# The last plain block of the down product: its loads tied to a place in the queue, its splits spaced otherwise, and the last scaling read from PSUM

## The chip, the cores and the metric

The kernel runs on 1 core of a Trainium2 chip. The metric is device time in microseconds (us), the median of 3 runs. TensorE (PE) multiplies, VectorE (DVE), ScalarE (ACT) and GpSimd (POOL) do everything elementwise, and every transfer is issued by SyncE (SP), in one queue and in order.

## The reference, cut to what matters

One step of a two-layer decoder. The first layer is a Mamba-2 mixer, the second is sliding-window attention, and each is followed by a squared-ReLU MLP. All is float32. The change touches the down product of the MLPs, the output product of the mixer (they share code) and the final norm.

```python
def rmsnorm(x, w):
    xf = x.astype(jnp.float32)
    xf = xf * lax.rsqrt(jnp.mean(xf * xf, axis=-1, keepdims=True) + EPS)
    return (xf * w.astype(jnp.float32)).astype(x.dtype)

def sq_relu_mlp(h, norm_w, w_up, w_down):
    return h + jnp.square(jax.nn.relu(rmsnorm(h, norm_w) @ w_up)) @ w_down
...
    y_prompt = rmsnorm(hp, final_norm_w)
    y_sample = rmsnorm(hs, final_norm_w)
```

## The kernel before, in words

The stream is kept transposed, features on the 128 partitions and tokens in columns (1104 columns in the first layer, 1088 in the second). A float32 operand is multiplied as two fp32r parts, hi and lo, with three matmuls per product (`mm3`, lines 204 to 206). To make the parts ("a split") ACT copies the tile to fp32r (hi) and DVE subtracts that from the tile (lo).

The down product sums over 4096 hidden features in blocks. The first and the last block of 512 features are plain products (`down_block`, tile `R0`, called R in the trace). The six tiles of features between them go as 4 blocks through `block_products`: seven products in place of eight for each 2x2 cut. A place in it is written (b, p, i): block b of 4 (of 2 in the mixer), weight group p of 4, product i of 7. Each (b, p) takes two loads of weights (`down_weights`, line 1160), which are added, subtracted and split (lines 1166 to 1172, 1047, 1048), and each product is added to the stream or to a sum by DVE (line 1264), which frees its PSUM bank. Each block needs seven split operands. They are loaded by `load` (line 1224) and split by `parts` (lines 1229, 1230) around the border of two blocks: a slot can be loaded again only when the block before has made its last product with it. Seven operands and the spare memory of R0 turn in a ring: the third block keeps two operands in R0, at its products i = 2 and i = 3 of p = 3.

The last block's `step` also fetches the data of the last plain block into R0: `last[0]` is `block_load`, four loads (line 1140) of a quarter each, numbered j = 0 to 3 here, and `last[1](j)` is `block_parts(j)`, the split of one quarter (ACT line 1145, DVE line 1146). The lo parts of quarters 0 and 1 lie where the second of the two operands in R0 was, those of 2 and 3 lie in memory that nothing uses during `block_products`; the hi parts of all four lie over the two operands.

The order on an engine is not the order of the text. The program is built with `schedule_with_timeline_sim=True`: a scheduler places each instruction, earlier in the text first, as soon as a model of the time says that its inputs and its memory are ready. `tc.issue_after(ins)` adds an edge of order alone: what the block issues on the engine of `ins` comes behind `ins` in its queue. It is used with `self.last_raw` in two places: the loads of the stream (line 1133) and one copy from memory to memory, `out_dram<-in_cache_v_dram` (line 1425). In the kernel before, `last_raw` is set by the up product's weight loads alone (line 1041).

At the very end the last plain block goes through `down(tail=2)`: the last four of eight feature tiles u are made chunk by chunk (three chunks c of 384, 384 and 320 columns), and `final` follows each tile: squares summed on ACT and DVE; `final_rs` sums over partitions with one-column matmuls (line 1726), takes root (1728) and reciprocal (1729) and makes diagonal matrices `dg` (1732); `final_bc` spreads the factor over the partitions with matmuls (1743) into PSUM and copies it to SBUF (`rs`, 1745); `final_scale` multiplies (1755 with the norm's weight as well, 1758 without) and stores (1759). For chunks 0 and 1 the eight multiplications go to POOL and DVE, four each; for chunk 2 to DVE six, to POOL two. POOL reads `rs` in SBUF. DVE reads `rs` too for chunks 0 and 1, and PSUM for chunk 2.

Of the kernel before, what the change touches and what calls it, by code (L numbers as in the profile page):

```python
# [93 lines left out]
class Stream:  # L94
# [29 lines left out]
    def load(self, X):  # L124

        self.X = X
        for c in self.rs:
            self.k.nc.sync.dma_start(out=X[:, :, self.cols(c)], in_=self.h_d[:, :, self.cols(c)])
        for c in list(self.rs):
            self.norm(c)  # L130
# [11 lines left out]
class Kernel:  # L142
# [1010 lines left out]
    def down_weights(self, view, p):  # L1153

        nc = self.nc
        sh = [KB, P]
        raws = []
        for j in range(2):
            t = self.np.tile([P, 2, KB, P], F32, tag="n3", bufs=2, name="raw") if p % 2 else self.raw([P, 2, KB, P])
            nc.sync.dma_start(out=t, in_=view[p, :, j])  # L1160
            raws.append(t)
        (a11, a12), (a21, a22) = ((t[:, 0], t[:, 1]) for t in raws)

        def add(a, b, op):
            t = self.np.tile([P] + sh, F32, tag="n1", bufs=5, name="s")
            nc.vector.tensor_tensor(out=t, in0=a, in1=b, op=op)
            return t
        yield self.wparts(a11, sh)
        s1 = add(a21, a22, ALU.add)
        yield self.wparts(s1, sh)  # L1170
        d = add(a11, a21, ALU.subtract)
        nc.vector.tensor_tensor(out=s1, in0=s1, in1=a11, op=ALU.subtract)  # L1172
        yield self.wparts(d, sh)
        yield self.wparts(s1, sh)
        yield self.wparts(a12, sh)
        yield self.wparts(a22, sh)
        yield self.wparts(add(a12, s1, ALU.subtract), sh)
# [55 lines left out]
    def block_products(self, w, big, us, slots, load, parts, free, make, last, more, early=(0, 0)):  # L1233


        nc = self.nc
        nn = us.shape[2]
        qw = nn // 2
        nb = len(slots)
        h = [[big[:, 4 * j:4 * j + 4, i * nn:i * nn + nn] for i in range(2)] for j in range(2)]  # L1240

        def step(b, p, i):

            if b == nb - 1:
                if (p, i) == (0, 0):
                    last[0]()
                if p > 0 and i == 2:
                    last[1](p - 1)
                if p == 3 and i == 5:
                    last[1](3)  # L1250
            else:
                for k in range(2):
                    if i == 0 and p == early[k]:
                        load(b + 1, k)
                if p in (1, 2) and i == 2:
                    parts(b + 1, p - 1)
                if p == 3 and i in free[b]:
                    load(b + 1, free[b].index(i) + 2)
                if p == 3 and i in make[b]:
                    parts(b + 1, make[b].index(i) + 2)  # L1260
            if p == 0 and b and i + 7 in make[b - 1]:
                parts(b, make[b - 1].index(i + 7) + 2)

        tt = lambda out, x, y: nc.vector.tensor_tensor(out=out, in0=x, in1=y, op=ALU.add)  # L1264
        for b in range(nb):
            for p in range(4):
                banks = {}
                hv = [[h[j][i][:, p] for i in range(2)] for j in range(2)]
                uv = us[:, p]
                for i, (wh, wl) in enumerate(self.down_weights(w[b], p)):  # L1270
                    e = self.CHAIN[p % 2][i]
                    new = e not in banks
                    if new:
                        banks[e] = self.pq.tile([P, 1024], F32, tag=e, bufs=1, name="m" + e)
                    x = [(hi[:, q], lo[:, q]) for hi, lo in slots[b][i] for q in range(lo.shape[1])]
                    for k in range(2):
                        cs = slice(k * qw, k * qw + qw)
                        self.mm3(banks[e][:, 512 + (k - 1) * qw:512 + k * qw], [(wh[:, q], wl[:, q]) for q in range(KB)],
                                 [(hi[:, cs], lo[:, cs]) for hi, lo in x], new)
                    pv = banks[e][:, 512 - qw:512 + qw]  # L1280
                    to = (uv, hv[1][1], hv[1][1], uv, hv[0][0], hv[1][0], hv[0][1])[i]
                    if i == 0 and b == 0:
                        nc.scalar.copy(out=uv, in_=pv)
                    else:
                        tt(to, pv, to)
                    if b == nb - 1 and i in (3, 4, 5):
                        e, to = ((nc.gpsimd, hv[1][1]), (nc.gpsimd, hv[0][1]), (nc.vector, hv[1][0]))[i - 3]
                        e.tensor_tensor(out=to, in0=to, in1=uv, op=ALU.add)
                    step(b, p, i)
                    more(b, p, i)  # L1290
# [445 lines left out]
    def final_bc(self, c, chs):  # L1736

        nc = self.nc
        n = chs[c][1]
        ps = self.gps()[:, :n]  # L1740
        for b in range(3):
            o = min(b * P, n - P)
            nc.tensor.matmul(out=ps[:, o:o + P], lhsT=self.ones_d, rhs=self.acc[c][:, b], start=True, stop=True)
        rs = self.fin("rs", 2, n)
        nc.scalar.copy(out=rs, in_=ps)
        self.acc[c] = {nc.gpsimd: rs, nc.vector: ps if c == 2 else rs}

    def final_scale(self, c, k, e, hts, chs):
        nc = self.nc
# [277 lines left out]
```

## Time and profile before

| | us |
|---|---|
| median of 3 runs | 2924.53 |
| lowest, highest | 2918.5, 2924.64 |
| profiled execution | 2923.57 |
| its span, first to last instruction | 2921.9 |
| PE busy in it | 2816.2 (96%) |
| DVE busy | 1895.0 (65%) |

Times in the trace count from the first instruction of the span. A row of a wait says who waited, for whom, how long in total, how often and how long at most. `x` is a count. Where PE has no row of a wait, it ran.

### The profile page before, as it was taken

To read this page: it belongs to the slowest core of one execution; us is meant where nothing else is said; L and a number is where in the kernel's file an instruction comes from. 1 tells how busy PE (TensorE), PEld (TensorE's weight loads), DVE (VectorE), ACT (ScalarE), POOL (GpSimd) and SP (SyncE) were. 2 spreads that over 40 slices of the span, in tenths; PEclk is the share of its full clock that TensorE was granted. 3 is DMA by queue.
4 is the path that set the end of the run, shared out by engine and by line. 5 is a ranking of instruction groups with operands and counts; after the bars stand their busy time and mean duration, and the time that the engine had idled before them with its cause. 6 is when DMAs were issued, how large, how long until landed. Compare 5 with 4: busy or idle time off the path is not lost.

```text
span 2921.9 us, 51729 instructions
## 1 busy us (share of the span) xinstructions
PE 2816.2 (96%) x19895; PEld 2711.0 (93%) x19895; DVE 1895.0 (65%) x2995; ACT 1413.9 (48%) x2742; POOL 1386.1 (47%) x1279
## 2 busy tenths in 40 slices
PE   8999999988989999999999999999999999999998
PEld 6999999978889999999999999988889999999998
DVE  6788777765657675455466765666678454356675
ACT  6555555544555264444343325655555444433333
POOL 5566666665546615444266573312112444345562
PEclk9999999999999999999999999999999999999998
DMA  3344544447655224444554422447453444533422
GB/s 137 91 128 124 125 128 123 123 123 258 218 206 171 80 85 149 136 156 139 224 212 171 161 89 94 160 153 261 164 187 133 150 140 150 206 138 124 151 96 73
DMA packets 219470, 433.43 MB, mean 148 GB/s; under 512 B 30728, under 2 KB 128392, under 8 KB 216648
## 3 DMA queue, kind: packets, MB, share of 16 engines
q1 hardware_dynamic: 219224, 430.14, 44.3%
q8 instruction: 156, 2.56, 0.4%
q14 instruction: 90, 0.74, 0.1%
HBM read 302.71 MB, written 128.32 MB: 148 GB/s over the span
## 4 chain that ended last, share of the span: by engine, by line
PE 77%; DVE 10%; ACT 4%; issue 3%; DMA 3%; POOL 3%; SPq 0%; DVEq 0%; ACTq 0%; POOLq 0%
PE g L204 10%; PE g L206 10%; PE g L205 10%; PE mc L204 4%; PE mc L206 3%; PE mc L205 3%; PE ma L204 3%; PE ma L205 3%; PE ma L206 3%; PE md L206 3%; PE md L205 3%; PE md L204 3%; PE mb L206 3%; PE mb L204 3%; PE mb L205 3%
## 5 line engine op out<-in xcount | busy, mean ns | idle before, releaser
L1048 POOL TENSOR_TENSOR w<-s,w 128x384 fp32r<-128x384 f32 (+1 forms) x272 | 370.4, 1368 | 386.9 <-ACT w L1047 354.4
L206 PE MATMUL g<-S,w 128*128 128x384 f32 (+2 forms) x1584 | 531.1, 336 | 3.9 <-POOL w L171 3.3
L204 PE MATMUL g<-S,w 128*128 128x384 f32 (+2 forms) x1584 | 533.4, 337 | 1.3 <-DVE qp L1462 0.6
L205 PE MATMUL g<-S,w 128*128 128x384 f32 (+2 forms) x1584 | 533.6, 337 | 0.0
L1048 POOL TENSOR_TENSOR w<-raw,w 128x384 fp32r<-128x384 f32 (+1 forms) x204 | 264.3, 1301 | 286.2 <-ACT w L1047 255.2
L171 POOL TENSOR_TENSOR w<-raw,w 128x1024 fp32r<-128x1024 f32 x96 | 247.1, 2574 | 253.3 <-ACT w L170 189.3
L206 PEld LDWEIGHTS g<-S,w 128*128 128x128 f32 x1584 | 301.9, 191 | 5.8 <-POOL w L171 3.6
L204 PEld LDWEIGHTS g<-S,w 128*128 128x128 f32 x1584 | 301.3, 190 | 4.7 <-issue 1.5
L205 PEld LDWEIGHTS g<-S,w 128*128 128x128 f32 x1584 | 301.7, 190 | 0.9 <-issue 0.3
L1047 ACT CAST w<-s 128x384 fp32r<-128x384 f32 (+1 forms) x272 | 149.8, 557 | 313.0 <-DVE s L1172 84.7
L204 PE MATMUL ma<-S,w 128*128 128x276 f32 (+1 forms) x808 | 235.2, 291 | 8.0 <-DVE us L1264 6.7
L206 PE MATMUL ma<-S,w 128*128 128x276 f32 (+1 forms) x808 | 234.7, 290 | 0.0
L205 PE MATMUL ma<-S,w 128*128 128x276 f32 (+1 forms) x808 | 234.3, 290 | 0.0
L1047 ACT CAST w<-raw 128x384 fp32r<-128x384 f32 (+1 forms) x204 | 111.8, 555 | 154.6 <-PE mc L206 45.2
L602 DVE SCALAR_TENSOR_TENSOR fm<-xp,cv,fm 128x1024 f32<-128x1024 f32 x96 | 162.8, 1698 | 33.1 <-ACT fm L583 32.5
L204 PEld LDWEIGHTS ma<-S,w 128*128 128x128 f32 x808 | 153.3, 190 | 9.3 <-ACT S L1229 2.7
L205 PE MATMUL g<-R,w 128*128 128x384 f32 (+2 forms) x480 | 158.6, 330 | 0.0
L204 PE MATMUL g<-R,w 128*128 128x384 f32 (+2 forms) x480 | 158.1, 329 | 0.0
L206 PE MATMUL g<-R,w 128*128 128x384 f32 (+2 forms) x480 | 158.1, 329 | 0.0
L205 PEld LDWEIGHTS ma<-S,w 128*128 128x128 f32 x808 | 153.5, 190 | 0.0
L206 PEld LDWEIGHTS ma<-S,w 128*128 128x128 f32 x808 | 153.2, 190 | 0.0
L170 ACT CAST w<-raw 128x1024 fp32r<-128x1024 f32 x96 | 100.5, 1047 | 105.8 <-DMA raw<-in_w_o_dram 19.9
(492 smaller groups left out, 8696.0 us busy)
## 6 DMA issues: line engine op xcount, KB each, us to landing
raw<-in_w_up_dram SPq DMA_DIRECT2D x64, 512.0 KB
raw<-in_w_in_dram SPq DMA_DIRECT2D x48, 512.0 KB
raw<-in_w_downs_dram SPq DMA_DIRECT2D x64, 384.0 KB
w<-ws_o SPq DMA_DIRECT2D x48, 512.0 KB
w<-ws_q SPq DMA_DIRECT2D x40, 512.0 KB
ab<-acs_d SPq DMA_DIRECT2D x64, 256.0 KB
S<-t_d SPq DMA_DIRECT2D x18, 828.0 KB
S<-t_e SPq DMA_DIRECT2D x18, 816.0 KB
```

Of the source, the lines that this page charges most:

```text
L170: nc.scalar.copy(out=wh, in_=raw)
L171: nc.gpsimd.tensor_tensor(out=wl, in0=raw, in1=wh.bitcast(F32), op=ALU.subtract)
L204: mm(out=out, lhsT=wh, rhs=xh, start=(first and k == 0), stop=False)
L205: mm(out=out, lhsT=wh, rhs=xl, start=False, stop=False)
L206: mm(out=out, lhsT=wl, rhs=xh, start=False, stop=(k == n - 1))
L602: nc.vector.scalar_tensor_tensor(out=acc[:, :SEQ], in0=xp[:, k:k + SEQ], scalar=cv[:, j, k:k + 1], in1=acc[:, :SEQ], op0=ALU.mult, op1=ALU ...
L1047: nc.scalar.copy(out=t[:, 0], in_=src)
L1048: nc.gpsimd.tensor_tensor(out=t[:, 1], in0=src, in1=t[:, 0].bitcast(F32), op=ALU.subtract)
```

## The change

The four loads of the last plain block move from (last b, 0, 0) to (last b, 1, 0), and get an edge of order behind `last_raw`, which is now also set by `down_weights`: there it is the second weight load of p = 1 of the last block. The four splits move from (1, 2), (2, 2), (3, 2), (3, 5) to (1, 3), (2, 2), (2, 5), (3, 2), in the form (p, i). The three callers of `block_products` (mixer, first and second layer) share this. In `final_bc`, DVE's factor is the tile in PSUM for every chunk.

```diff
             t = self.np.tile([P, 2, KB, P], F32, tag="n3", bufs=2, name="raw") if p % 2 else self.raw([P, 2, KB, P])
-            nc.sync.dma_start(out=t, in_=view[p, :, j])
+            self.last_raw = nc.sync.dma_start(out=t, in_=view[p, :, j]).ins
...
             if b == nb - 1:
-                if (p, i) == (0, 0):
-                    last[0]()
-                if p > 0 and i == 2:
-                    last[1](p - 1)
-                if p == 3 and i == 5:
-                    last[1](3)
+                if (p, i) == (1, 0):
+
+                    with self.tc.issue_after(self.last_raw):
+                        last[0]()
+                if p > 0 and i in ((3,), (2, 5), (2,))[p - 1]:
+                    last[1](p - 1 if i < 4 and p < 3 else p)
...
         nc.scalar.copy(out=rs, in_=ps)
-        self.acc[c] = {nc.gpsimd: rs, nc.vector: ps if c == 2 else rs}
+        self.acc[c] = {nc.gpsimd: rs, nc.vector: ps}
```

## Rows read from the trace of the kernel before

**Rows 1.** The page, busy time of each engine, share of span, instructions

```profile
PE 2816.2 (96%) x19895; PEld 2711.0 (93%) x19895; DVE 1895.0 (65%) x2995; ACT 1413.9 (48%) x2742; POOL 1386.1 (47%) x1279
```

**Rows 2.** Waits of PE in 860:1000, 1400:1760, 2560:2922: total us, times, longest

```profile
PE mc L204 <- DVE hh L1264: 1.8, 2, 1.0
...
PE ma L204 <- DVE us L1264: 4.9, 2, 2.5
PE mb L204 <- DVE hh L1264: 4.8, 1, 4.8
PE ma L204 <- DVE hh L1264: 3.4, 3, 1.2
...
PE g L1743 <- DVE dg L1732: 4.4, 2, 3.5
PE mb L204 <- DVE hh L1264: 2.6, 1, 2.6
...
PE ma L204 <- DVE us L1264: 1.8, 2, 0.9
...
PE md L205 <- DVE S L1230: 1.1, 1, 1.1
```

**Rows 3.** Timeline of SP's queue, 2586:2592 and 2766:2812: start us, us, line, transfer

```profile
2588.95 0.36 SPq L1140 DMA_DIRECT2D R<-r_e  x1
...
2768.25 2.58 SPq L1160 DMA_DIRECT2D raw<-in_w_downs_dram  x2
2771.18 2.35 SPq L1224 DMA_DIRECT2D A<-t_e  x2
2777.72 0.93 SPq L1140 DMA_DIRECT2D R<-r_e  x2
```

**Rows 4.** Timeline of ACT around the last block's start, layer 2 (2775:2784), layer 1 (1650:1664)

```profile
2775.46 1.11 ACT L1145 CAST R<-R 128x1088 fp32r<-128x1088 f32 x1 [1.56 <-PE mc L205]
...
2781.57 1.11 ACT L1145 CAST R<-R 128x1088 fp32r<-128x1088 f32 x1 [0.26 <-DMA R<-r_e]
2782.89 1.11 ACT L1145 CAST R<-R 128x1088 fp32r<-128x1088 f32 x1 [0.21 <-DMA R<-r_e]
...
1656.83 1.58 ACT L1229 CAST A<-A 128x1656 fp32r<-128x1656 f32 x1 [4.87 <-DMA A<-t_d]
```

**Rows 5.** Groups of DVE by form, 2775:2811: count, busy us, mean ns, idle before

```profile
L1146 DVE TENSOR_TENSOR R<-R 128x1088 fp32r<-128x1088 f32 x4 | 6.7, 1695 | 0.3 <-ACT R L1145 0.3
```

**Rows 6.** Groups of DVE by form in the final norm, 2890:2922

```profile
L1755 DVE SCALAR_TENSOR_TENSOR hh<-hh,nv,rs 128x384 f32<-128x384 f32 x4 | 5.5, 1407 | 0.8 <-ACT rs L1745 0.8
L1758 DVE TENSOR_TENSOR hh<-hh,rs 128x384 f32<-128x384 f32 x4 | 5.3, 1355 | 0.0
...
L918 DVE TENSOR_TENSOR hh<-hh,g 128x384 f32<-128x384 f32 x3 | 1.7, 553 | 1.7 <-PE g L206 1.5
...
...
L1755 DVE SCALAR_TENSOR_TENSOR hh<-hh,nv,g 128x320 f32<-128x320 f32 x2 | 1.0, 546 | 1.9 <-ACT rs L1745 1.9
```

**Rows 7.** Timelines of DVE and ACT at the end (2896:2918, 2899:2916)

```profile
2911.94 0.16 DVE L1729 RECIPROCAL rt<-rt 128x3 f32<-128x3 f32 x1
...
2909.03 0.26 ACT L1728 ACTIVATE rt<-g,eps 128x3 f32<-128x3 f32 x1 [2.30 <-PE g L1726]
```

**Rows 8.** Timeline of PE at the end (2902.8:2915)

```profile
2902.57 0.31 PE L206 MATMUL g<-R,w 128*128 128x320 f32 x1
2903.83 0.94 PE L1743 MATMUL g<-dg,ones_r 128*128 128x128 f32 x6 [0.94 <-DVE dg L1732]
2906.31 0.54 PE L1726 MATMUL g<-ones_r,acc 128*128 128x1 f32 x2 [1.55 <-DVE acc L1705]
...
2912.48 1.65 PE L1743 MATMUL g<-dg,ones_r 128*128 128x128 f32 x6 [3.49 <-DVE dg L1732]
```

**Rows 9.** Stretch 2906.5:2912: busy us of PE, PEld, DVE, ACT, POOL, granted clock, DMA

```profile
2906.50:2912.00 5.50, 2.49 (x12) 2.40 (x12) 5.24 (x5) 0.49 (x2) 4.80 (x4) 0.50 0.29 105
```

**Rows 10.** Timeline of SP's queue, 1366:1373

```profile
1368.28 0.86 SPq L1425 DMA_DIRECT2D out_dram<-in_cache_v_dram  x1
```

## The prediction

> **What bounds the kernel now.** I read the page first, then PE's waits stage by stage, then the queues around the longest waits. PE is busy 96% of the span [rows 1], so time is won only where PE stands still, or after its last product. The waits in the three stages that the change touches are few [rows 2]. Ahead of the last block of `block_products` PE waits 1.8 us in the mixer, 4.8 + 1.2 = 6.0 in the first layer (1.2 is the longest of three in its row) and 2.6 + 1.1 = 3.7 in the second, together 11.5 us. All end with DVE: it adds a product to the stream too late to free a bank, or splits an operand too late. The borders between earlier blocks, which have seven splits but none of R, cost 2.5 + 1.1 = 3.6 us each in the first layer and at least 0.9 each in the second. So DVE is short of time at every border, and the four splits of R, 6.7 us of DVE at the last one in the second layer [rows 5], come on top there. The second place is the end: PE waits twice for `dg`, 4.4 us [rows 2], and the reciprocal ahead of it starts at 2911.94, although the root that it takes ended at 2909.29 [rows 7]. In between DVE multiplied chunk 1.
>
> **The factor from PSUM.** Four multiplications of 384 columns by DVE per chunk stay, for chunks 0 and 1; their second operand moves from SBUF to PSUM. They take 1.407 and 1.355 us now, beside POOL, which multiplies from SBUF in the same time (4.80 us for its four). An addition of the same 384 columns with one operand in PSUM takes 0.553, and a multiplication with the weight, 320 columns, 0.546, also beside POOL [rows 6, 9]. I take 0.553 for two and 0.546 x 384/320 = 0.655 for the other two: 2.4 us a chunk in place of 2 x 1.407 + 2 x 1.355 = 5.5. The start does not move: chunk 2, which reads PSUM already, waits 1.9 us for ACT's copy all the same [rows 6]. The PSUM bank is held 2.4 us instead of one copy, and comes round again only seven tiles later, after the products in between: no cost while those last longer.
>
> On the path it counts in two steps. Chunk 0: its multiplications end 3.1 us sooner, and the additions of chunk 2's tiles behind them on DVE move up with them, until they meet the products themselves. PE's last product ends at 2902.88; one addition of at most 0.55, one square on ACT of about as much, and the last sums can start at some 2904.0 in place of 2906.31 [rows 6, 8]: 2.3 us. Chunk 1: its four then end before the root of chunk 2 does, so the reciprocal follows the root at once: 2911.94 - 2909.29 = 2.65 us [rows 7]. Behind them all is as before: diagonals, matmuls, copy, DVE's six, stores. Sum: 4.95 us. POOL does not come late: its 4.80 us [rows 9] start 2.3 us sooner too and end near 2909.4, ahead of chunk 2's copy. The lower bound is 2.65, if chunk 0 gains nothing. Upwards: in the last stretch the granted clock is 0.50 of full speed, that is 1.2 GHz, after PE had idled 0.94 and 1.55 us, and six matmuls that took 0.94 us at 2903.83 take 1.65 at 2912.48 [rows 8, 9]. With shorter idling it may stay at 2.4 GHz longer; 0.7 for these six and about 1.2 for the twelve ahead of them give an upper bound of 6.9.
>
> The Trainium skill speaks against this edit: "VectorE: DVE Perf Modes", section "Rules for kernel authors", says to accept the plain rate from PSUM, or to copy to SBUF first if many operations read it. By that rule the copy that the kernel makes anyway should be read, and the edit would gain nothing. The row of 0.553 against 1.355 says otherwise, and "SBUF — State Buffer", section "SBUF: two separate sides", has a reason: a DVE instruction with two SBUF inputs and GpSimd share a port that one holds for a whole instruction.
>
> **The loads and splits.** What decides is whether the splits leave the border. The order is not the text's. Quarters 2 and 3, written into the last block, are loaded at 2588.95, about 190 us ahead, as soon as their memory is free (the other one follows); and the first split runs at 2775.46, at the very moment PE finishes with the operand under its hi part, though the text has all four in the second to fourth group of the last block, which has not begun then [rows 3, 4]. So the place in the text is only a rank among what is ready, and I expect nothing of the new places by themselves. What binds is the edge. But the load it points to is early: weights are fetched almost two groups ahead, and the second weight load of (last, p = 1) is the second of the pair at 2768.25 to 2770.83. Quarters 0 and 1 are at 2777.72 anyway, when their memory comes free [rows 3]. So their loads stay, and so may their splits, which ACT starts at 2781.57 and 2782.89 as the data lands [rows 4]. Only quarters 2 and 3 move, from 2589 to just after 2770.83, into the stretch where the operands of the last block are loaded (from 2771.18). They are needed once the operands above them are done, 2775.46 for the first.
>
> Price of that: two quarters land 1.32 us apart [rows 4], so up to 2.6 us of transfer stand ahead of the first operand loads. If these are late and DVE has nothing else to do, it costs up to 2.6 us a place; if the scheduler, seeing the data later, puts the splits of quarters 2 and 3 behind the last block's operands, it gains up to half of the four splits, 3.4 us, where PE waits that long. I take 0, since in the second layer the transfers have slack and DVE, not the data, is late; ends -2 and +2.5 over the three places. The early transfers that vanish (2588.95) lie where PE has no wait: nothing. The weights of p = 2 are issued behind these loads on SP and have a whole group of time: nothing; without that cover, one quarter's 1.3 us.
>
> One more transfer moves. `last_raw` now is the last weight load of the first layer's down product, so the copy out of `in_cache_v`, at 1368.28 now [rows 10], can be issued only behind that, between the last weights of that product and those of the plain block. It takes SP 0.86 us; no instruction waits for it. Nothing, or that 0.86 if it stood before an urgent load.
>
> **How the numbers follow.** The profiled execution took 2923.57 us (span 2921.9), 1 us under the median, so the sum is set against the median: 2924.5 - 5.0 = 2919.5.
>
> **Rivals.** First, the end is shortened and the splits stay: 2919.5, own range 2916 to 2922.5, chance 0.52.
>
> Second, the splits do leave the border, because the later data lets the scheduler keep all four behind the operands. Then the waits fall to those of borders without R: 6.0 to 3.6, 3.7 to about 1, the mixer's 1.8 to 0, 6.9 us more, at best all 11.5. Time 2912.5, from 2908 to 2916. For it: the splits are what the last border has beyond the others. Against: quarters 0 and 1 keep their moment. 0.25.
>
> Third, slower: the loads of quarters 2 and 3 stand ahead of the operands at all three places. In the first layer ACT already stands 4.87 us until an operand has landed [rows 4], so there every us of transfer is one of lateness; DVE starts later into the crowd and PE pays in full. 3 x 2.6 = 7.9, less 5.0: 2927.5, and up to 2933 if the order of DVE's queue gets worse as well. It decides where ACT's split of the first operand waits for its load longer than now. 0.15.
>
> Fourth, the PSUM factor gives nothing, by the rule above, as DVE would be as slow from PSUM as beside POOL, and the border is unchanged: 2924. 0.08.
>
> From these: faster by over 0.2% (below 2918.7; 0.2% is about what a measurement of this kernel can tell from no change): two fifths of the first, 0.21, and nearly all of the second, 0.24: 0.45. Slower by over 0.2% (above 2930.4): 0.07. Within: 0.48. The range, from well into the second case to near the third, leaves a tenth on each side: 2909.5 to 2926.
>
> **What would show it.** Right: DVE's four multiplications of chunks 0 and 1 near 0.55 to 0.65 us; the last sums starting some 1.1 us after PE's last product; the reciprocal right behind the root. Quarters 2 and 3 loaded right behind a pair of weights, 0 and 1 between two operand loads as now, and PE's waits at the three borders still there, within 2 us. Wrong: multiplications above 1 us; POOL as the last before the stores; the splits of R behind the last operand's split (second case); ACT's wait for the first operand at a border longer than 4.87 us (third case).

## The result and the profile after

The changed kernel takes 2930.26 us (median of 14 runs, 2924.49 to 2932.12) where the kernel before takes 2923.07 in the same session: a ratio of 1.0020, 95% interval 1.0013 to 1.0028. (A ratio here is the one on record from the runs of both kernels in one session; it is not the quotient of the two medians, which would be 1.0025.) The forecast was 2919.5, in a range from 2909.5 to 2926. The time went up, and it lies above the range. The profiled execution has a span of 2930.4 us.

PE has hardly more to do than before [rows 1]; it waits more. The page's busy times of the changed kernel:

```profile
PE 2818.2 (96%) x19895; PEld 2711.7 (93%) x19895; DVE 1896.8 (65%) x2995; ACT 1417.4 (48%) x2742; POOL 1387.3 (47%) x1279
```

PE's waits in it, in 860:1000 (the mixer), 2200:2300 (end of the second layer's up product) and 2560:2935 (its down product and the final norm); columns as in [rows 2]:

```profile
PE mc L204 <- DVE hh L1264: 2.8, 1, 2.8
PE mb L204 <- DVE us L1264: 1.8, 1, 1.8
...
PE mc L204 <- DVE rx L1077: 2.2, 1, 2.2
...
PE g L1743 <- DVE dg L1732: 2.1, 2, 2.0
...
PE ma L204 <- DVE hh L1264: 1.4, 1, 1.4
```

The mixer's last border costs PE 4.6 us of waiting in place of 1.8 [rows 2]. The 2.2 us for `rx` are new, and so are the 1.4 us for `hh` (the first border of the second layer). In the final norm the wait for `dg` went from 4.4 to 2.1 [rows 2], the one for `acc` from 1.55 [rows 8] to 0.50 (PE's rows further down). SP's queue of the changed kernel, around the mixer's last border, the second layer's first and its last:

```profile
928.04 0.33 SPq L1224 DMA_DIRECT2D A<-z_d  x1
928.41 4.99 SPq L1140 DMA_DIRECT2D R<-g_d  x4
...
2598.95 0.91 SPq L1224 DMA_DIRECT2D R<-t_e  x2
...
2783.52 0.36 SPq L1224 DMA_DIRECT2D A<-t_e  x1
2783.92 0.91 SPq L1140 DMA_DIRECT2D R<-r_e  x2
2785.77 0.32 SPq L1224 DMA_DIRECT2D A<-t_e  x1
2790.28 1.53 SPq L1140 DMA_DIRECT2D R<-r_e  x2
```

In the second layer two quarters of R now come behind the weights of p = 1, as forecast, but behind the first operand's load and not ahead of it; the other two stand between two operand loads as before, and the early one of [rows 3] is gone. In the mixer all four quarters now stand behind one operand.

### The profile page after: what moved, and what is told of

It reads as the page before. It is cut to its first block, busy times and chain, and to the rows that moved or that the text cites. A ratio compares the mean times of both kernels' runs of the same rounds, so it can differ in the third digit from the quotient of the medians.

```text
span 2930.4 us, 51724 instructions
## 1 busy us (share of the span) xinstructions
PE 2818.2 (96%) x19895; PEld 2711.7 (93%) x19895; DVE 1896.8 (65%) x2995; ACT 1417.4 (48%) x2742; POOL 1387.3 (47%) x1279
## 4 chain that ended last, share of the span: by engine, by line
PE 77%; DVE 8%; issue 5%; DMA 4%; ACT 3%; POOL 3%; SPq 0%; DVEq 0%; POOLq 0%; ACTq 0%
PE g L204 10%; PE g L205 10%; PE g L206 10%; PE mc L204 4%; PE mc L206 3%; PE mc L205 3%; PE ma L204 3%; PE ma L205 3%; PE ma L206 3%; PE md L206 3%; PE md L205 3%; PE md L204 3%; PE mb L204 3%; PE mb L206 3%; PE mb L205 3%
## 5 line engine op out<-in xcount | busy, mean ns | idle before, releaser
L204 PE MATMUL mc<-S,w 128*128 128x276 f32 (+1 forms) x512 | 149.1, 291 | 3.7 <-DVE rx L1077 2.2
```

Of the source, the lines that this page charges most:

```text
L204: mm(out=out, lhsT=wh, rhs=xh, start=(first and k == 0), stop=False)
```

## How the stages of the traces were compared

Each matmul of the trace of before has its counterpart in every other trace. The difference of their start times, and how far it grows over a stretch, tells what that stretch lost or gained (negative) against before; times are those of the trace of before, and the end is what lies behind 2860. All values in us:

| kernel | 690 to 915, untouched | mixer's last border, 915 to 1000 | up end, layer 2, 2190 to 2310 | first border, layer 2, 2580 to 2640 | last border, layer 2, 2740 to 2860 | end |
|---|---|---|---|---|---|---|
| changed kernel | +2.4 | +5.5 | +3.9 | +1.6 | +0.5 | -4.5 |
| the same again (after_again) | +0.1 | +4.1 | +1.2 | +1.5 | +0.2 | -4.5 |
| psum_only | +0.2 | +0.1 | +0.1 | 0.0 | +0.6 | -4.5 |
| loads_only | +2.0 | +5.8 | +2.2 | +1.6 | +1.8 | 0.0 |
| no_edge | +1.9 | -0.2 | +0.6 | 0.0 | +0.5 | -4.4 |
| own_mark | +1.8 | +5.8 | +1.6 | +1.5 | +1.7 | -4.5 |
| mixer_only | +1.9 | +5.8 | -0.4 | 0.0 | +0.1 | -4.5 |
| no_mixer | +2.0 | -0.1 | +2.1 | +1.7 | -0.4 | -4.5 |
| splits_late | +2.0 | +5.0 | +0.3 | +0.1 | +0.1 | -4.5 |
| edge_p2 | +0.1 | +4.5 | +2.4 | +1.6 | -0.4 | -4.5 |
| edge_p3 | +2.0 | +3.8 | +2.2 | +1.9 | +1.0 | -4.5 |
| second_later | +0.1 | -0.1 | +1.8 | +0.8 | +1.2 | -4.5 |
| pool_split | +2.1 | +2.3 | +2.0 | 0.0 | +2.6 | -4.8 |
| psum_second | +2.0 | -0.2 | +1.5 | 0.0 | +0.8 | -4.5 |
| up_fixed | 0.0 | +6.0 | +1.1 | +1.5 | +0.5 | -4.4 |

The first column warns: it holds no edit, and it shows 0 or 2 us. Two traces of the changed kernel differ there by 2.3 and in all by 8.7 us of span (2930.4 and 2921.7); the first was taken of the slowest of that kernel's 14 executions, the second of the fastest of after_again's 11. What goes with the two values is where PE's granted clock falls. The order of work on PE, DVE, ACT and POOL is the same there, but in every trace of the 0 group the clock falls to 0.50 near 783, in every one of the 2 us group near 808 in its place, and there the lag to before grows. (In before it is 0.50 over 783.4 to 786.6 and 1.00 over 805 to 812; in own_mark it is 1.00 over 782 to 786 and 0.50 over 809.2 to 812.4.) Which is cause and which effect, and what sends a trace into one group or the other, isn't shown. So a single trace doesn't settle 2 us in a stage; a column in which the kernels fall into two groups by their edit does. The first layer's borders (1500 to 1780, not shown) scatter from -1.8 to +1.6 in the kernels with either loading and show no such groups; second_later has +1.4 there, psum_second +2.5 and pool_split +3.7.

## Experiments: the two parts apart

**psum_only** is the kernel before with the last line of the change alone; **loads_only** has the rest.

```diff
-        self.acc[c] = {nc.gpsimd: rs, nc.vector: ps if c == 2 else rs}
+        self.acc[c] = {nc.gpsimd: rs, nc.vector: ps}
```

Expected of psum_only: 

> The factor of chunks 0 and 1 from PSUM alone, loads and splits as before. Theory A (the two parts are independent; the final norm gives what the two traces show at their ends, and all of the loss lies at the last plain block's loads): 3.5 to 5 us under the kernel before, some 2919, with DVE's four multiplications of a chunk near 0.55 us each and PE's two waits in the final norm 2 us shorter together. Theory B (the PSUM factor gives nothing, and the shorter end in the trace after is noise of one execution): within 1 us of before, 2923.

Expected of loads_only: 

> The loads and splits of the change alone; the final norm as before. Theory A (independent parts): 7.2 + 3.5 to 5 = 10.5 to 12 us above before, some 2934; the mixer's last border some 5 us longer, new waits of about 2 us at the end of the second layer's up product and of 1.4 us at the second layer's first border. Theory B (the loss lies in the final norm or in single executions): under 4 us above before.

Measured: 2919.62, ratio 0.9982 (0.9973 to 0.9991), and 2936.18, ratio 1.0035 (1.0021 to 1.0049). Theory A of both held. The parts add: -0.18% and +0.35% make +0.17%, against +0.20% (0.13 to 0.28). The end is 4.5 us shorter in every trace with that line and unchanged in loads_only. DVE's multiplications of chunks 0 and 1 by form, in the changed kernel (2895:2935):

```profile
L1755 DVE SCALAR_TENSOR_TENSOR hh<-hh,nv,g 128x384 f32<-128x384 f32 x4 | 2.3, 611 | 0.8 <-ACT rs L1745 0.8
...
L1758 DVE TENSOR_TENSOR hh<-hh,g 128x384 f32<-128x384 f32 x4 | 2.0, 548 | 0.0
```

They take 0.61 and 0.55 us in place of 1.41 and 1.36 [rows 6]. So the loss lies in the loads and splits, 10 us of it by loads_only.

**no_edge** has all of the change but the edge; **own_mark** has the edge to a mark of its own, so that `last_raw`, and the copy out of `in_cache_v` with it, stays where it was.

```diff
                 if (p, i) == (1, 0):
-                    with self.tc.issue_after(self.last_raw):
-                        last[0]()
+                    last[0]()
```

```diff
-            self.last_raw = nc.sync.dma_start(out=t, in_=view[p, :, j]).ins
+            self.last_down = nc.sync.dma_start(out=t, in_=view[p, :, j]).ins
...
-                    with self.tc.issue_after(self.last_raw):
+                    with self.tc.issue_after(self.last_down):
```

Expected of no_edge: 

> The whole change without the edge: loads at (1,0) in the text, splits at the change's new places, PSUM factor. Theory A (the place in the text is only a rank; the edge alone moves anything): as psum_only, 2919.6 within 1 us. Theory B (the places count too): 2 to 4 us above it.

Expected of own_mark: 

> The whole change, but the edge points to a mark of its own, so that the copy out of in_cache_v stays behind the up product's last load as before. Theory A (that copy costs nothing): as the changed kernel, 2930 within 1 us, and the waits at the end of the second layer's up product still there. Theory B (the copy holds SP up at an urgent load): 1 to 3 us under the changed kernel.

Measured: 2918.41, ratio 0.9979 (0.9970 to 0.9988), and 2929.7, ratio 1.0022 (1.0013 to 1.0030). Theory A of both held, no_edge a little below its number. Without the edge the new places in the text do nothing, and the copy costs nothing. The loss needs the edge.

## Experiments: which of the three places

**mixer_only** has the change's loads, edge and split places only where there are two blocks (the mixer), and the kernel before's in the layers. **no_mixer** is the changed kernel, but with the loads at their old place and without the edge in the mixer; its edit:

```diff
-                if (p, i) == (1, 0):
-                    with self.tc.issue_after(self.last_raw):
-                        last[0]()
+                if (p, i) == ((0, 0) if nb == 2 else (1, 0)):
+                    if nb > 2:
+                        with self.tc.issue_after(self.last_raw):
+                            last[0]()
+                    else:
+                        last[0]()
```

Expected of mixer_only: 

> PSUM factor; the change's loads, edge and split places in the mixer alone, as before in the two layers. Theory A (the mixer's loss is its own and stays to the end): psum_only + 8, some 2927.5, with PE's waits of 4.7 us at the mixer's last border. Theory B (part of the difference between the changed kernel and no_mixer comes from the layers): 2923 to 2925.

Expected of no_mixer: 

> The whole change, except that in the mixer's down product (two blocks) the last plain block is loaded at (0,0) with no edge, as before. Theory A (the mixer's border is where most is lost: PE waits 4.7 instead of 1.8 us there, and the clock falls): 5 us under the changed kernel, some 2925. Theory B (the mixer's longer border is given back behind it, as the lag between the traces falls by itself later): as the changed kernel, 2929 to 2930.

Measured: 2925.47, ratio 1.0006 (0.9997 to 1.0015), and 2922.24, ratio 0.9996 (0.9987 to 1.0005). Against psum_only the mixer's edge costs 0.24% and the layers' edges 0.14%; both together, less 0.18%, make the +0.20% of the changed kernel (each ratio is good to 0.09%). So most of the loss is the mixer's, and a third comes from the layers. Of mixer_only theory B was nearer: its cause is there, and 2925.47 is just above its 2923 to 2925, while theory A's 2927.5 was too much. no_mixer came out below theory A's 2925: theory A took the mixer's part for 5 us, and 0.24% is 7. Theory B fell. In the table the mixer's part is one stretch, its last border, and the layers' part is two that the diff's lines don't name: the end of the second layer's up product and its first border.

## Experiments: why the mixer's border costs 5.5 us

DVE at that border in psum_only, where loads and order are those of the kernel before (start us, us, operation, idle time before):

```profile
927.27 0.73 DVE L1264 TENSOR_TENSOR hh<-mb,hh 128x552 f32<-128x552 f32 x1 [3.83 <-PE mb L206]
928.29 1.31 DVE L1146 TENSOR_TENSOR R<-R 128x1104 fp32r<-128x1104 f32 x1 [0.29 <-ACT R L1145]
929.56 0.73 DVE L1264 TENSOR_TENSOR hh<-mc,hh 128x552 f32<-128x552 f32 x1
930.33 1.32 DVE L1146 TENSOR_TENSOR R<-R 128x1104 fp32r<-128x1104 f32 x1
...
933.04 1.89 DVE L1230 TENSOR_TENSOR A<-A 128x1656 fp32r<-128x1656 f32 x1 [0.47 <-ACT A L1229]
```

Here, other than in the second layer, two of the four splits (L1146) run ahead of the crowd, in gaps in which DVE otherwise waits for PE. They can, because their quarters were loaded some 30 us earlier (SP issues them at 899.89 and 902.91). With the edge they can't. Two theories remain for the price: two more splits in the crowd, or two more transfers ahead of the operands. **splits_late** tells them apart: psum_only, loads as early as before, but in the mixer ACT's part of the splits is queued behind its split of the operand A.

```diff
-                nc.scalar.copy(out=hi, in_=lo.bitcast(F32))
+                self.op_split[b, i] = nc.scalar.copy(out=hi, in_=lo.bitcast(F32)).ins
...
-                    last[1](p - 1)
+                    with self.tc.issue_after(self.op_split[1, 2]) if nb == 2 else ExitStack():
+                        last[1](p - 1 if i == 2 else 3)
```

Expected: 

> As psum_only, loads of R as early as before; but in the mixer the four splits of R are queued on ScalarE behind the split of the operand A at the last border, where the changed kernel has them. It tells the transfers from the place of the splits. Theory A (the mixer's loss is that two splits leave idle stretches of VectorE ahead of the border and enter the crowd): PE waits there 4 to 5 us instead of 1.9, and the loss of mixer_only, 4 to 5.5 us, is there without any late load: 2924 to 2925. Theory B (the loss is two more transfers ahead of the operands): as psum_only, 2919.6 within 1 us.

Measured: 2924.53, ratio 1.0001 (0.9993 to 1.0010), 0.19% above psum_only, and +5.0 us at that border. Its DVE there, and PE's waits in 900:1000:

```profile
928.84 0.73 DVE L1264 TENSOR_TENSOR hh<-mc,hh 128x552 f32<-128x552 f32 x1 [1.56 <-PE mc L206]
931.93 1.88 DVE L1230 TENSOR_TENSOR A<-A 128x1656 fp32r<-128x1656 f32 x1 [2.36 <-ACT A L1229]
...
934.38 3.34 DVE L1146 TENSOR_TENSOR R<-R 128x1104 fp32r<-128x1104 f32 x2
```

```profile
PE mb L204 <- DVE hh L1264: 3.9, 1, 3.9
PE md L205 <- DVE S L1230: 1.1, 1, 1.1
PE mc L204 <- DVE hh L1264: 0.5, 1, 0.5
```

DVE idles 1.56 and 2.36 us where it split before, and then has all four. PE waits 5.5 us in place of 1.9. No load of R or of an operand is late in this kernel, so the splits' place is enough for the loss, as theory A said; that the late loads add something isn't shown. The waits are only 2.9 us (mixer_only: 3.05 + 1.74, less the 1.88 of psum_only) of the 5.8 lost there. The stretch 925:975 in mixer_only (PE busy, granted clock, DMA share, GB/s):

```profile
925.00:975.00 50.00, 45.22 (x328) 0.93 0.46 171
```

and in psum_only:

```profile
925.00:975.00 50.00, 48.02 (x373) 1.00 0.43 148
```

PE's clock falls from 2.4 to 1.2 GHz twice in that stretch, each time just behind one of the two long waits, which end at 946.05 and 956.73; in before and psum_only it stays at 1.00 there. Pieces of both low stretches in mixer_only, each with one as long behind it (the same columns):

```profile
947.30:950.60 3.30, 3.30 (x15) 0.50 0.02 5
950.70:954.00 3.30, 3.30 (x28) 1.00 0.00 0
957.50:960.80 3.30, 3.30 (x17) 0.50 0.00 0
961.00:964.30 3.30, 3.30 (x28) 1.00 0.00 0
```

PE is busy throughout and makes 13 and 11 matmuls fewer at the low clock. By the 0.118 us that one takes behind, that is 2.8 us (an estimate from these rows), nearly the whole remainder of 2.9. In splits_late the clock falls once, 0.97 over 925:975, and 1.4 us of the 5.0 are left beyond the waits. So in mixer_only half of the loss is PE waiting, and the other half is the clock that falls behind the waits.

## Experiments: do the splits leave the border, and is that a gain

**edge_p3** and **edge_p2** load all quarters behind the weights of p = 3 or p = 2, at all three places, and split them there; PSUM factor as in the change.

```diff
+                if (p, i) == (3, 0):
+                    with self.tc.issue_after(self.last_down):
+                        last[0]()
+                if (p, i) in ((3, 2), (3, 3), (3, 4), (3, 5)):
+                    last[1](((3, 2), (3, 3), (3, 4), (3, 5)).index((p, i)))
```

Expected of edge_p3: 

> PSUM factor as in the change; all four quarters loaded behind the weights of p = 3 at all three places, split at (3,2), (3,3), (3,4), (3,5), behind the last block's own operands. Theory A (the splits in the crowd are what the last border costs beyond the others): PE waits there fall to those of borders without R, the mixer's to about 0, the first layer's from 6.0 to 3.6, the second's from 3.7 to about 1: up to 6.9 us under psum_only, some 2913. Theory B (what costs is that the early loads vanish and the order of the rest shifts with them, as in no_mixer): the new waits of 2 us at the end of the second layer's up product and of 1.5 us at its first border are there again, and what the last borders give is eaten up: 2919 to 2922.

Expected of edge_p2: 

> As edge_p3, but the loads behind the weights of p = 2, splits at (2,3), (2,5), (3,2), (3,5). Theory A: as the weights are fetched almost two groups ahead, these loads are still ahead of the border's end; the splits leave it in part: 3 to 5 us under psum_only, some 2916. Theory B: as the changed kernel without its mixer's loss, 2920 to 2923.

Measured: 2932.37, ratio 1.0031 (1.0019 to 1.0042), and 2924.77, ratio 1.0001 (0.9992 to 1.0010). In edge_p3 the splits do leave the border, and it is the slower of the two. DVE in the mixer, and the waits of PE in 860:1000 that it has in place of those of psum_only:

```profile
953.67 3.35 DVE L1166 TENSOR_TENSOR s<-raw 128x384 f32<-128x384 f32 x2
...
967.12 1.30 DVE L1146 TENSOR_TENSOR R<-R 128x1104 fp32r<-128x1104 f32 x1
969.34 0.56 DVE L1172 TENSOR_TENSOR s<-s,raw 128x384 f32<-128x384 f32 x1 [0.91 <-POOL w L1048]
969.81 2.16 DVE L1146 TENSOR_TENSOR R<-R 128x1104 fp32r<-128x1104 f32 x1
```

```profile
PE ma L204 <- DVE hh L1263: 4.2, 2, 2.2
```

The splits now stand among the weight sums of the next group, over 35 us later than in psum_only, and one of the two waits is there, ending at 979.12. The other ends at 957.81, behind two weight sums (953.67) and ahead of every split of R. So the border keeps a wait of 2.2 us without these splits, where psum_only waits 1.9 with them. Theory A of both fell, and so did theory B in its numbers: 2919 to 2922 for edge_p3, and for edge_p2 a total without the mixer's loss, which it has (+4.5). With its work at the border DVE is late there; with it elsewhere it is late elsewhere. The table doesn't close for these two: its stages without the first add up to +4.4 for edge_p3 and +3.6 for edge_p2, the ratios to +9 and +0.3. Where that rest lies isn't known.

**pool_split** takes the work from DVE altogether: as psum_only, but POOL makes the lo parts of R.

```diff
-        nc.vector.tensor_tensor(out=lo, in0=lo.bitcast(F32), in1=hi.bitcast(F32), op=ALU.subtract)
+        (e or nc.vector).tensor_tensor(out=lo, in0=lo.bitcast(F32), in1=hi.bitcast(F32), op=ALU.subtract)
```

Expected: 

> As psum_only, but the low parts of the four quarters of R (L1146) are made by GpSimd instead of VectorE, at all three places. Theory A (these four splits on VectorE are what the last border costs beyond the others, whatever they are loaded by): up to 6.9 us under psum_only, some 2913 to 2916. Theory B (the wait only goes over to GpSimd, which makes the low parts of the weights): PE waits for POOL w at the borders, 2919 to 2925.

Measured: 2930.64, ratio 1.0023 (1.0014 to 1.0033): 0.41% above psum_only, worse than either theory said. Operations by form at the second layer's last border (2775:2815), first POOL and then DVE in pool_split:

```profile
L1146 POOL TENSOR_TENSOR R<-R 128x1088 fp32r<-128x1088 f32 x4 | 10.7, 2686 | 1.7 <-ACT R L1145 1.7
```

```profile
L1230 DVE TENSOR_TENSOR A<-A 128x1632 fp32r<-128x1632 f32 x2 | 6.6, 3310 | 0.0
```

and DVE in psum_only:

```profile
L1146 DVE TENSOR_TENSOR R<-R 128x1088 fp32r<-128x1088 f32 x4 | 7.5, 1899 | 0.3 <-ACT R L1145 0.3
...
L1230 DVE TENSOR_TENSOR A<-A 128x1632 fp32r<-128x1632 f32 x2 | 3.7, 1846 | 0.0
```

DVE is rid of 7.5 us, but its splits of the operands, from SBUF beside a POOL that works from SBUF, take 3.31 us each in place of 1.85. PE then waits 5.8 us at once for DVE (`hh`), not for POOL. The Trainium skill, "SBUF — State Buffer", section "SBUF: two separate sides", has DVE with two SBUF inputs and GpSimd share a port; the rows agree. That stretch loses 2.6 us, the mixer's 2.3, and the first layer's borders 3.7.

## Experiments: the loss in the layers

At the second layer's first border the kernel before issues two loads of R's quarters between and behind two operand loads. SP's queue there in psum_only:

```profile
2587.60 0.32 SPq L1224 DMA_DIRECT2D R<-t_e  x1
2588.04 0.36 SPq L1140 DMA_DIRECT2D R<-r_e  x1
2588.49 0.38 SPq L1224 DMA_DIRECT2D R<-t_e  x1
2588.93 0.72 SPq L1140 DMA_DIRECT2D R<-r_e  x1
```

and DVE behind it:

```profile
2595.33 0.72 DVE L1264 TENSOR_TENSOR hh<-md,hh 128x544 f32<-128x544 f32 x1
2596.15 0.73 DVE L1264 TENSOR_TENSOR hh<-mc,hh 128x544 f32<-128x544 f32 x1
2596.85 2.14 DVE L1230 TENSOR_TENSOR R<-R 128x1632 fp32r<-128x1632 f32 x1
```

In no_mixer the two operand loads follow each other (as in the changed kernel at 2598.95, above), and the second split has gone ahead of an addition (lines are shifted by 2):

```profile
2597.80 0.72 DVE L1266 TENSOR_TENSOR hh<-md,hh 128x544 f32<-128x544 f32 x1
2598.43 2.05 DVE L1230 TENSOR_TENSOR R<-R 128x1632 fp32r<-128x1632 f32 x1
2600.40 0.71 DVE L1266 TENSOR_TENSOR hh<-mc,hh 128x544 f32<-128x544 f32 x1
```

All that DVE has behind it is late, and PE waits 1.5 us at this border, where psum_only doesn't wait. All seven kernels that load R late in the layers, with operand loads untouched, lose 1.5 to 1.9 us there; those without lose none. **second_later** queues the second operand's load of the next block behind the weights of p = 2, in the layers of no_mixer; **psum_second** does that to psum_only.

```diff
-                    if i == 0 and p == early[k]:
-                        load(b + 1, k)
+                    if i == 0 and p == (early[k] if nb == 2 else 2 * k):
+                        with self.tc.issue_after(self.last_raw) if nb > 2 and k else ExitStack(): load(b + 1, k)
```

Expected of second_later: 

> As no_mixer, but in the two layers the load of the second operand of the next block is queued behind the second weights of p = 2, so that the two operand loads no longer stand next to each other at a border. Theory A (with the early loads of R gone, the second operand lands next to the first and its split goes ahead of an addition that frees a bank): the wait of 1.5 us at the second layer's first border is gone and the total falls by 1.5 to 3, to 2919 to 2921; the wait of 2 us at the end of that layer's up product, of which this changes nothing, stays. Theory B (the wait has another cause): as no_mixer, 2922.

Expected of psum_second: 

> As psum_only, with the second operand's load of each next block in the layers behind the second weights of p = 2. Theory A (splits that stand in the crowd at the beginning of a border move back to where VectorE is idle, at every border of the layers): 1 to 4 us under psum_only, 2916 to 2918.5. Theory B (the waits at those borders are set by the weights' sums, and the later split comes late itself): 2919.6 or more.

Measured: 2923.85, ratio 0.9997 (0.9988 to 1.0006), and 2923.12, ratio 0.9988 (0.9979 to 0.9997). At that border the wait falls from 1.5 to 0.5 us and the stretch's loss from 1.7 to 0.8: the cause holds there for the larger part. In total nothing is won, against theory A of both, and psum_second is no better than psum_only: the same edit sits at every border of both layers. That it makes others worse is likely but not clear of the scatter (first layer: +1.4 in second_later and +2.5 in psum_second; second layer's last border: +1.2 in second_later, -0.4 in no_mixer).

The end of the second layer's up product loses 1.1 to 3.9 us in all kernels with the late loads in the layers, and 1.5 and 2.0 in psum_second and pool_split, which shift other work. Among the kernels without either it is -0.4 to +0.6. Its DVE queue in the changed kernel shows

```profile
2265.76 3.21 DVE L1057 TENSOR_TENSOR s<-raw 128x512 f32<-128x512 f32 x2 [0.15 <-DMA raw<-in_w_up_dram]
2268.90 0.71 DVE L1077 TENSOR_TENSOR rx<-mc,rx 128x544 f32<-128x544 f32 x1
```

two weight sums ahead of an addition that stands behind nothing in psum_only (2257.74, its sums at 2258.38). **up_fixed** turns that order back in the changed kernel, and nothing else (`r3` is the addition); **after_again** is the changed kernel on the same chip.

```diff
-        s1 = add(a21, a22, ALU.add)
+        with self.tc.issue_after(self.r3) if (layer, f) == (1, 3) else ExitStack(): s1 = add(a21, a22, ALU.add)
...
-        d = add(a11, a21, ALU.subtract)
+        with self.tc.issue_after(self.r3) if (layer, f) == (1, 3) else ExitStack(): d = add(a11, a21, ALU.subtract)
```

Expected of up_fixed: 

> The changed kernel with one edit: in the second layer's up product two sums of weights (L1057) are queued on VectorE behind the addition of a product (L1077), the order of the kernel before; nothing else moves on any engine. Theory A (the new wait of 2.2 us at the end of that stage is the order of these instructions on VectorE, which the scheduler drew otherwise): the wait is gone and the total 2 us under the changed kernel, some 2928. Theory B (the wait comes from something else, such as the clock or the weights' transfer): as the changed kernel, 2930.

Expected of after_again: 

> The changed kernel itself, beside up_fixed on the same chip: 2930 within 1 us by every theory, with the waits of its first trace (4.7 us at the mixer's last border, 2.2 at the end of the second layer's up product, 1.4 at its first border).

Measured: 2928.76, ratio 1.0019 (1.0010 to 1.0028), and 2928.5, ratio 1.0013 (1.0004 to 1.0022). Theory A fell: its number is near, but the changed kernel beside it takes as little. after_again itself is 1.5 us under what was expected, and in its trace the waits are 4.9 us at the mixer's last border, 1.0 at the end of the up product and 1.3 at the first border. In up_fixed the wait of DVE's `rx` is gone, and PE waits there for ACT:

```profile
PE ma L204 <- ACT rx L1103: 0.9, 1, 0.9
```

On ACT's queue the activation that frees that bank is also later than before, and this edit doesn't touch it. So the stage loses 1.1 us with DVE's order put back and 1.2 without. The 3.9 of the first trace of the changed kernel are the same order and a longer wait (2.2 in place of 1.0), with a lower clock behind it (the changed kernel, same columns):

```profile
2271.20:2274.50 3.30, 3.30 (x16) 0.50 0.02 5
```

In after_again the clock stays at 1.00 behind the shorter wait, with 28 matmuls in as long a stretch (2264.5 to 2267.8); the 12 fewer are 1.4 us by the 0.118 us of one there (an estimate). That the scheduler drew this stage otherwise is seen; which of its orders costs what, and which layer's edge brings them about, stays open.

## Why the prediction failed, point by point

- **Factor from PSUM: right in size.** 4.95 forecast, 4.5 in the traces, 5.3 by psum_only's ratio. Its steps, in the changed kernel (PE at the end, and the granted clock under the last sums):

```profile
2917.08 0.35 PE L1726 MATMUL g<-ones_r,acc 128*128 128x1 f32 x2 [0.50 <-DVE acc L1705]
...
2920.52 0.79 PE L1743 MATMUL g<-dg,ones_r 128*128 128x128 f32 x2 [1.97 <-DVE dg L1732]
2921.47 1.22 PE L1743 MATMUL g<-dg,ones_r 128*128 128x128 f32 x4 [0.16 <-DVE dg L1732]
```

```profile
2917.10:2918.50 1.40, 1.40 (x12) 1.00 0.06 13
```

  The last sums start 1.17 us behind PE's last product, which ends at 2915.91, in place of 3.43: 2.26 won, 2.3 forecast. From there to the `dg` matmuls it is 3.44 in place of 6.17 [rows 8]: 2.73 won, 2.65 forecast. That these two agree is partly luck, as three things went otherwise and nearly cancel. The twelve sums ran at 2.4 GHz, not at 1.2 [rows 9], and were 1.2 us shorter, which the forecast had in its upper bound alone. The root so came sooner, and DVE's four multiplications did not end before it, as was said: the reciprocal comes 0.6 us behind the root. And the three diagonals, now beside POOL, take 1.99 us in place of 0.68, where the forecast had them as before. The six matmuls then take 2.17 in place of 1.65. 2.26 + 2.73 - 0.52 = 4.47. By the fourth rival, the rule of the Trainium skill to copy to SBUF first ("VectorE: DVE Perf Modes", section "Rules for kernel authors"), the edit would have given nothing; the rows disagree (0.61 and 0.55 us from PSUM, 1.41 and 1.36 from SBUF beside POOL), and the measurement decides.
- **New places in the text: nothing. Right** (no_edge). **The moved copy: nothing. Right** (own_mark).
- **Loads and splits: 0, from -2 to +2.5 over the three places. Wrong**, and here the forecast fell: it was about +10 us (loads_only 1.0035). The step that failed is the one that carried the second layer's rows over to all three places. [rows 3] and [rows 4] show splits that wait for PE and start at the border; so it seemed indifferent whether their data come 190 us ahead or just in time. In the mixer, of whose queues the prediction shows no row, two of the four splits ran in DVE's gaps ahead of the border. That cover was the thing to price: 2 x 1.3 us of DVE pushed into the crowd, 5.5 us lost, half of it by waits and half by the clock that fell behind them. Also wrong, without a price that the runs show: the two quarters do not stand ahead of the first operand's load at any of the three places, but behind it.
- **"The early transfers that vanish: nothing". Wrong.** They cost PE nothing as transfers, but they parted two operand loads, and with that kept a split behind an addition: 1.5 us at the second layer's first border. The scheduler's orders shifted in the up product too (1.1 us and more).
- **The borders in the layers, where the edge sits: right** that nothing is won or lost within what the traces can tell (-0.4 to +1.8 at the second layer's).
- **First rival: fell. Second rival (the splits leave the border, 2912.5): wrong as a price.** edge_p3 makes it happen and takes 2932. The waits at borders with R are not made of R's splits alone: the border keeps 2.2 us of waiting without them, and PE waits again where they went.
- **Third rival (slower, 2927.5): right side and near in size, by another cause.** It was to act by late transfers at all three places. In the first layer its sign came, ACT's wait for the first operand grew from 4.87 [rows 4] to 5.59 (the changed kernel, the row below), without a loss that the traces show; in the mixer splits_late has the loss with no load late. Its 0.15 was too low, since the bound it went by (2.6 us a place) was that of the transfers and not that of DVE's work.

```profile
1664.10 1.58 ACT L1229 CAST A<-A 128x1656 fp32r<-128x1656 f32 x1 [5.59 <-DMA A<-t_d]
```

In all: 5.5 (mixer) + 1.6 (first border) + 1.2 to 3.9 (up end) - 4.5 = +3.8 to +6.5, and the ratios 1.0013 and 1.0020 are +3.8 and +5.8. The upper end holds a fall of the clock that the second trace doesn't have. The best kernel here is neither of the two: the one line of psum_only (0.9982), or the same with the new places and no edge (0.9979), beats both; the two can't be told apart.

## What to carry to other kernels

Work that is ready early and has no deadline fills the gaps of a busy engine; loading its data just in time takes these gaps away, and the work meets the crowd. Before an edge is tied to a place that several callers share, look at the queue at each of them, and at what vanishes from the early place too. Where an order is drawn by a scheduler, an edit moves instructions far from its lines, so read all stages, and in more than one trace.

## What was not expected of the hardware

- Two traces of one program differ by 8.7 us of span. In 690 to 915, where all have the same order of work, traces fall into two groups, 0 and 2 us, by where the granted clock falls: near 783 or near 808.
- PE lost 5.8 us where it waited 2.9 us longer: behind the waits its granted clock fell to 0.50 twice (15 and 17 matmuls in 3.3 us, in place of 28), and that is nearly all of the other 2.9.
- Beside subtractions by POOL from SBUF, 2.69 us each, DVE's of 1632 columns take 3.31 us in place of 1.85.
